# The sample's high and low parts side by side in one stationary operand

## The chip, the cores and the metric

The kernel runs on one core of a Trainium2 chip. The metric is the device time of one execution in microseconds (us). An execution is one inference step of one layer, for a prompt of 2048 frames and a sample of 64 frames that continues a running stream.

## The reference

A layer takes each frame of 1024 numbers, normalises it, and multiplies it with one wide input matrix. Its columns feed two branches and their gates. Branch A is a differential attention with four heads, branch B a retention with four heads. Both are gated, projected, merged and projected once more. Cut to what matters here:

```python
def layer_inputs(x, norm_g, w_in, b_gate, qn_g, kn_g):
    h = rmsnorm(x, norm_g) @ w_in              # (rows, 1024) @ (1024, W_IN)
    qa, ka, va, za, qb, kb, vb, zb, ga, gb = jnp.split(h, _split_points(), axis=-1)
    ...
def layer_output(x, oa, ob, za, zb, ga, gb, subln_g, lam_init, w_oa, w_ob, w_out):
    oa = (rmsnorm(oa, subln_g) * (1.0 - lam_init)).reshape(B, T, W_A) * jax.nn.silu(za)
    ob = rmsnorm(ob).reshape(B, T, W_B) * jax.nn.silu(zb)
    m = ga * (oa @ w_oa) + gb * (ob @ w_ob)
    return x + m @ w_out
def reference(...):
    # the same layer for the prompt (2048 rows) and for the sample (64 rows),
    # with the sample's attention over 4096 cached frames and its own 64
```

The outputs are y for prompt and sample, their attention keys and values, and the retention states.

## The kernel before, in words

Everything is float32. TensorE multiplies in a rounded form of it (F32R), so every operand is kept as a high part and a low part: the high part is the number rounded to that form, the low part is the rest. A product is three matmuls that add up in one accumulator: high times high, high times low and low times high. Low times low is left out.

A matmul has a stationary operand, which is loaded into the array (rows are the contraction, columns the rows of the output), and a moving operand, up to 512 columns wide. The accumulator is a bank of 128 partitions with 512 numbers each; its partitions are the stationary operand's columns.

The frames are taken in tiles of 128 rows. `x_tile` (L369) transposes a tile on TensorE and writes its high part `xh` (ScalarE) and its low part `xl` (VectorE), with eight contraction tiles of 128. The prompt's first half gives eight tiles; the sample is the ninth, with 64 rows. It stands in the columns 512 to 576 of the second segment.

There are two ways to project. In `natural` (L587) and `opening` (L510) the frames are stationary and the weights move, so the output has frames in its partitions. This is done for the values, keys and queries of the attention and for the values of the retention. In `transposed` (L749) the weights are stationary and the frames move. In both ways `mm_group` (L491) issues the three matmuls of each of the eight contraction tiles. For the attention's three projections in the first half of the frames the weights are 512 columns wide; for the retention's values there are two groups that are 256 wide. The sample is the last tile of each, with its 64 rows as 64 stationary columns: 24 matmuls in a group.

When a tile's matmuls are issued, an epilogue is started as a task of its own: `fin_qk` (L616), `fin_va` (L696) or `fin_vb` (L733). It reads the bank on ScalarE and VectorE, gives the bank (`mm`, two of them) back, and stores by DMA. The weights come by DMA in pieces of 256 KB (`ws`, three buffers); ScalarE makes the high part (L462) and GpSimd nearly all of the low parts (L472).

The last stage goes through eight groups of 256 prompt frames. `m_tile` (L1612) and `m_fin` (L1641) make the merged branches, as high and low part, for 256 columns of the prompt and eight of the sample; L1667 to L1670 collect the sample's eight in `self.ms`. `y_tile` (L1672) then multiplies a tile of 128 frames with the output matrix in two halves of 512 columns (two banks of `at`), three matmuls for each contraction tile (L1698 to L1700), and `y_fin` (L1707) adds the input and stores. After the eight groups one more `y_tile` does the sample, from `self.ms`.

The order of the work on TensorE, ScalarE and VectorE is set when the kernel is built: tasks run as coroutines under a clock that is estimated from each instruction's size, and the task of highest rank that is ready by that clock issues next. A buffer is taken with `take` and given back with `give` and an estimated time. Each engine carries out its instructions in the order in which they were issued. The order on GpSimd and on SyncE, which issues all the DMAs, is set by the framework's scheduler.

Of the kernel before, what the change touches and what calls it, by code (L numbers as in the profile page):

```python
# [60 lines left out]
class Hybrid:  # L61
# [307 lines left out]
    def x_tile(self, j, wait=True, mid=None):  # L369
        nc = self.nc  # L370
        yield lambda: len(self.xq) > j and self.xq[j] is not None
        xt, t, r, seg, col = self.xq[j]
        if wait:
            yield t
        self.until(t)
        for q in range(2):
            tag = "tp" if q == 0 else "pv"
            yield from self.take(tag)
            tp = self.psum(tag)
            for c in range(4):  # L380
                nc.tensor.transpose(tp[:, c * r:(c + 1) * r],
                                    xt[:, (4 * q + c) * 128:(4 * q + c + 1) * 128],
                                    self.ident[:r, :r])
# [4 lines left out]
            nc.scalar.copy(hi, pv)  # L388
            nc.vector.tensor_sub(lo, pv, hi.bitcast(F32))  # L389
# [101 lines left out]
    def mm_group(self, ps, n, us, wsl, x, wfirst, last, between=None):  # L491
        nc = self.nc
        seg, xsl = x
        for c in range(KC):
            a, b, _, tags, _ = yield from self.w_unit(us, c)
            a, b = a[:, wsl], b[:, wsl]
            xh, xl = self.xh[seg][:, c, xsl], self.xl[seg][:, c, xsl]
            ops = ((a, xh), (a, xl), (b, xh)) if wfirst else ((xh, a), (xh, b), (xl, a))
            for i, (p, q) in enumerate(ops):
                nc.tensor.matmul(ps, p, q, start=c == 0 and i == 0, stop=c == KC - 1 and i == 2)  # L500
                self.P(n)
            if last:
                for tag in tags:
                    self.give(tag, self.pe + LAT)
            if c % 2 and c < KC - 1:
                yield self.pe
                if between:
                    yield from between(c)

    def opening(self, fin):  # L510
# [4 lines left out]
        self.x_alloc(0)  # L515
        self.x_alloc(1)
        us, low = [], []
        yield lambda: len(self.xin) > 0
# [45 lines left out]
        for j in range(1, 9):  # L564
            def between(c):
# [4 lines left out]
                if c == 3 and j + 1 < 9:  # L570
# [4 lines left out]
                    if j + 2 < 9:  # L575
# [3 lines left out]
            yield from self.take("mm")  # L579
            ps = self.psum("mm")  # L580
            self.until(self.xt_ready[j])
            yield from self.mm_group(ps[:r], 512, us, slice(0, 512), (seg, slice(col, col + r)), False,
                                     j == 8, between)
            self.spawn(fin(ps[:r], r, 1, 128 * j if j < 8 else T, self.pe + LAT), 0, "w")
            yield self.pe

    def natural(self, half, fin, fresh=False, wide=False):  # L587
# [6 lines left out]
        for j0 in range(0, len(tiles), per):  # L594
# [3 lines left out]
            for u, (src, r, seg, col) in enumerate(group):  # L598
                if fresh:
                    yield lambda: len(self.xt_ready) > j0 + u  # L600
                    yield self.xt_ready[j0 + u]
                yield from self.mm_group(ps[:r, n * u:n * u + n], n, us, slice(0, n),
                                         (seg, slice(col, col + r)), False, j0 + u == len(tiles) - 1)
# [3 lines left out]
            self.spawn(fin(ps[:r, :n * len(group)], r, len(group), t0, self.pe + LAT), 0, "w")  # L607
            yield self.pe

    def rows_out(self, dst, src, nu, nbytes):  # L610
# [5 lines left out]
    def fin_qk(self, which, g, nh=2):  # L616
# [3 lines left out]

        def fin(ps, r, nu, t0, t):
            n, ng, rt = 128 * nh * nu, 2 * nh * nu, r * nu
# [11 lines left out]
            else:  # L634
                nc.vector.tensor_mul(raw3, ps.rearrange("p (g d) -> p g d", d=64),
                                     self.gk[:r].unsqueeze(1).to_broadcast([r, ng, 64]))
                t2 = self.V(n, t)
            self.give("mm", max(t1, t2))
            yield t1
# [56 lines left out]
    def fin_va(self, g, nh=2):  # L696
# [3 lines left out]

        def fin(ps, r, nu, t0, t):
            n, rt = 128 * nh * nu, r * nu
# [11 lines left out]
            t3 = self.V(n, t1)  # L714
            self.give("mm", max(t2, t3))
            if t0 < T:
# [16 lines left out]
    def fin_vb(self, g):  # L733
        nc = self.nc
        ep = self.ep

        def fin(ps, r, nu, t0, t):
            n, rt = 256 * nu, r * nu
# [3 lines left out]
            t = self.A(n, t)  # L742
            self.give("mm", t)
            yield t
# [896 lines left out]
    def m_fin(self, g, ct, pss):  # L1641
# [24 lines left out]
        yield t2 + 2000  # L1666
        for d, m in zip(self.ms, (h, l)):  # L1667
            nc.vector.tensor_copy(d[:, ct, 8 * g:8 * g + 8], m[:, 256:GW])
            t2 = self.V(8)
        self.msn.append(t2)  # L1670

    def y_tile(self, g, sel, r, x, y):  # L1672
# [3 lines left out]
        for nh in range(2):  # L1676
            nsl = slice(512 * nh, 512 * nh + 512)
            yield from self.take("xt")
            xt = self.sb(pb, [128, 512], "xt", "oxt")[:r]
            tx = self.ld(xt, x[:, nsl], 2048 * r)  # L1680
            yield from self.take("at")
            run.append((nsl, xt, tx, self.psum("at")[:r]))
        first = 8 if sel is None else 7
        order = [(c, k) for k in range(2) for c in range(first)] + [(c, k) for c in range(first, 8) for k in range(2)]
        for ct, nh in order:
            nsl, xt, tx, ps = run[nh]
            yield lambda: len(self.wout) > ct and nh in self.wout[ct][2] and len(self.mq[g]) > ct
            h, l, t = self.mq[g][ct]
            if sel is None:
                yield lambda: len(self.msn) == 64  # L1690
                t = max(t, self.msn[-1])
                h, l = self.ms[0][:, ct, :], self.ms[1][:, ct, :]
            else:
                h, l = sel(h), sel(l)
            wh, wl, tw = self.wout[ct]
            if max(t, tw[nh]) > self.pe:
                yield max(t, tw[nh])
            nc.tensor.matmul(ps, h, wh[:, nsl], start=ct == 0, stop=False)  # L1698
            nc.tensor.matmul(ps, h, wl[:, nsl], start=False, stop=False)  # L1699
            nc.tensor.matmul(ps, l, wh[:, nsl], start=False, stop=ct == 7)  # L1700
            for _ in range(3):
                t = self.P(512)
            yield self.pe
            if ct == 7:
                self.spawn(self.y_fin(ps, xt, y[:, nsl], r, max(t, tx)), 0)

# [12 lines left out]
    def out_stream(self):  # L1719
# [16 lines left out]
    def w_stream(self):  # L1736
# [53 lines left out]
        self.z4 = self.es.enter_context(self.tc.tile_pool(name="p3b", bufs=1))  # L1790
        self.ms = [self.z4.tile([128, 8, 64], F32R, tag=f"ms{j}", name=f"ms{j}") for j in range(2)]
        self.spawn(self.out_stream(), 8)
# [139 lines left out]
```

## Time and profile before

| | us |
|---|---|
| Median of 3 runs | 1988.08 |
| Lowest and highest | 1986.14, 1988.54 |
| The profiled execution | 1990.07 |
| Its span in the profile | 1988.3 |

The profile is of one execution. Its span runs from the first to the last instruction. A row of the timeline gives the start in the span, the duration, the engine, the line of the kernel, the operation, the tiles (output, then inputs), the shapes, a count, and in brackets how long the engine was idle before and for whom. Matmuls overlap, so a matmul's duration is longer than the distance to the next start; that distance, the step, is what counts for a busy TensorE. "128\*64" is the stationary operand: 128 contraction rows, 64 columns. A row of a group gives a count, then busy time in us and the mean of one in ns, then idle time before the group and who ended it. A row of DMA issues gives the count, the size of one and the median time from issue to landing. PE is TensorE, PEld its loads of stationary operands, DVE VectorE, ACT ScalarE, POOL GpSimd, SPq the queue of SyncE.

### The profile page before, as it was taken

The page shows a single profiled execution, that of the slowest core. Times are in us where ns is not written, and L with a number is a line of the kernel's source. Part 1 is how long each engine was busy: PE and PEld are TensorE (multiplying, and loading weights), DVE is VectorE, ACT ScalarE, POOL GpSimd, SP SyncE. Part 2 cuts the span into 40 slices and gives each one's busy share as a digit, 9 for nine tenths or more (in the row PEclk, how much of TensorE's full clock was granted, in tenths as well). Part 3 has the DMA queues.
Part 4 walks back from the last instruction along what each step waited for, and adds up shares of the span by engine and source line. Part 5 has one row for each costly group of instructions (what it writes and reads, how often), then busy time and mean ns, then how long its engine had stood idle before and what let it go on. Part 6 is the DMA issues. An engine that isn't in the chain of part 4 may idle for free.

```text
span 1988.3 us, 34106 instructions
## 1 busy us (share of the span) xinstructions
PE 1963.8 (99%) x12206; PEld 1754.7 (88%) x12206; DVE 1057.2 (53%) x2786; ACT 991.0 (50%) x2185; POOL 417.3 (21%) x383
## 2 busy tenths in 40 slices
PE   9999999999999999999999999999999999999999
PEld 7778989998998989999998888888888888889997
DVE  6453665446565326547756656525644356444432
ACT  6432666655454436436757656635744544333330
POOL 2310121212121221221111111211122434222210
PEclk9999999999999999999999999999999999999999
DMA  7646553335665756664352342652233666444431
GB/s 245 200 143 177 138 157 118 117 87 152 174 174 152 174 151 196 200 187 137 102 153 81 109 137 62 175 146 85 70 98 114 202 219 206 141 130 148 131 93 53
DMA packets 332508, 285.21 MB, mean 143 GB/s; under 512 B 65905, under 2 KB 297329, under 8 KB 332338
## 3 DMA queue, kind: packets, MB, share of 16 engines
q1 hardware_dynamic: 332338, 283.03, 48.5%
q8 instruction: 96, 1.57, 0.3%
q14 instruction: 74, 0.61, 0.1%
HBM read 187.19 MB, written 91.49 MB: 140 GB/s over the span
## 4 chain that ended last, share of the span: by engine, by line
PE 64%; DVE 2%; DMA 2%; ACT 1%; issue 0%; POOL 0%; SPq 0%; POOLq 0%; ACTq 0%; DVEq 0%
PE mm L500 31%; PE at L1698 3%; PE at L1699 3%; PE at L1700 3%; PE s L956 2%; PE s L957 2%; PE at L1063 2%; PE mm L1630 2%; PE s L1632 2%; PE mm L1631 2%; PE mm L1632 2%; PE s L1631 2%; PE s L1630 2%; PE pv L1043 1%; PE pv L1042 1%; PE pv L1041 1%
## 5 line engine op out<-in xcount | busy, mean ns | idle before, releaser
L500 PE MATMUL mm<-xh,wh 128*128 128x512 f32 (+2 forms) x1280 | 459.3, 359 | 2.8 <-ACT ev L770 2.8
L500 PE MATMUL mm<-xh,wl 128*128 128x512 f32 (+2 forms) x1280 | 452.4, 353 | 0.0
L500 PE MATMUL mm<-xl,wh 128*128 128x512 f32 (+2 forms) x1280 | 451.8, 353 | 0.0
L472 POOL TENSOR_TENSOR wl<-ws,wh 128x512 fp32r<-128x512 f32 x189 | 258.6, 1381 | 867.2 <-ACT wh L462 605.5
L500 PE MATMUL mm<-wh,xh 128*128 128x256 f32 (+3 forms) x864 | 273.5, 317 | 0.3 <-DVE tlo L713 0.3
L500 PEld LDWEIGHTS mm<-xh,wh 128*128 128x128 f32 x1280 | 241.4, 189 | 32.4 <-ACT ev L770 3.3
L500 PEld LDWEIGHTS mm<-xh,wl 128*128 128x128 f32 x1280 | 241.1, 188 | 31.9 <-POOL wl L472 0.4
L500 PE MATMUL mm<-wh,xl 128*128 128x256 f32 (+3 forms) x864 | 267.9, 310 | 0.1
L500 PE MATMUL mm<-wl,xh 128*128 128x256 f32 (+3 forms) x864 | 267.6, 310 | 0.0
L500 PEld LDWEIGHTS mm<-xl,wh 128*128 128x128 f32 x1280 | 241.6, 189 | 27.8
L1078 DVE TENSOR_TENSOR atl<-at,ath 128x512 fp32r<-128x512 f32 (+1 forms) x144 | 93.9, 660 | 159.2 <-ACT ath L1076 159.2
L500 PEld LDWEIGHTS mm<-wh,xh 128*128 128x128 f32 (+1 forms) x864 | 162.8, 188 | 11.8 <-PE s L957 0.4
L500 PEld LDWEIGHTS mm<-wl,xh 128*128 128x128 f32 (+1 forms) x864 | 162.9, 189 | 11.0
L500 PEld LDWEIGHTS mm<-wh,xl 128*128 128x128 f32 (+1 forms) x864 | 162.8, 188 | 10.9 <-DVE xl L389 0.6
L770 ACT COPY ev<-mm 128x512 f32<-128x512 f32 x140 | 71.3, 510 | 191.4 <-PE mm L500 166.4
L995 ACT ACTIVATE row<-row,a_mx 128x1024 f32<-128x1024 f32 (+7 forms) x160 | 153.3, 962 | 17.5 <-DVE a_mx L975 16.3
L965 DVE CUSTOM_DVE_ANT_0 row<-s,dfar 128x512 f32<-128x512 f32 (+2 forms) x192 | 118.2, 631 | 57.7 <-PE s L957 57.1
L462 ACT CAST wh<-ws 128x512 fp32r<-128x512 f32 x192 | 115.4, 618 | 33.2 <-PE mm L500 22.0
L1076 ACT CAST ath<-at 128x512 fp32r<-128x512 f32 (+1 forms) x144 | 78.6, 562 | 100.1 <-PE at L1063 95.2
L956 PE MATMUL s<-K,q 128*128 128x512 f32 (+3 forms) x320 | 118.3, 374 | 4.2 <-DVE a_acc L965 4.2
L957 PE MATMUL s<-K,q 128*128 128x512 f32 (+3 forms) x320 | 115.5, 362 | 0.0
L1016 DVE SCALAR_TENSOR_TENSOR row<-row,a_w 128x1024 f32<-128x1024 f32 (+4 forms) x96 | 102.6, 1074 | 21.5 <-ACT row L1013 21.4
(220 smaller groups left out, 3998.0 us busy)
## 6 DMA issues: line engine op xcount, KB each, us to landing
ws<-in_w_in_dram SPq DMA_DIRECT2D x192, 256.0 KB, 3.2
q<-qT SPq DMA_DIRECT2D x128, 128.0 KB, 3.0
V<-vN SPq DMA_DIRECT2D x24, 512.0 KB, 4.8
K<-kT SPq DMA_DIRECT2D x48, 256.0 KB, 4.1
gt<-gaT SPq DMA_DIRECT2D x64, 132.0 KB, 2.1
gt<-gbT SPq DMA_DIRECT2D x64, 132.0 KB, 2.1
xt<-in_x_prompt_dram SPq DMA_DIRECT2D x16, 512.0 KB, 5.9
kn<-in_cache_k_T_dram SPq DMA_DIRECT2D x32, 256.0 KB, 3.7
```

Source lines behind the costliest of these rows:

```text
L462: self.nc.scalar.copy(h, st)
L472: self.nc.gpsimd.tensor_sub(l, st, h.bitcast(F32))
L500: nc.tensor.matmul(ps, p, q, start=c == 0 and i == 0, stop=c == KC - 1 and i == 2)
L956: nc.tensor.matmul(ps, q1s, kk, start=True, stop=False)
L957: nc.tensor.matmul(ps, q2s, kk, start=False, stop=True)
L965: nc.vector.tensor_tensor_reduce(out=units[k0 // 1024][:, k0 % 1024:k0 % 1024 + n], in0=ps, in1=tab, scale=-SLOPES[h], scalar=3.0e38, op0= ...
L995: nc.scalar.activation(u, u, AF.Exp, bias=mx, scale=-1.0, accum_out=lp[:, k:k + 1])
L1016: nc.vector.scalar_tensor_tensor(out=u0, in0=u0, scalar=w[:, 0:1], in1=u1, op0=ALU.mult, op1=ALU.add)
L1078: nc.vector.tensor_sub(al[:, :w], at[:, :w], ah[:, :w].bitcast(F32))
L1630: nc.tensor.matmul(ps, wh[:, csl], oh, start=kt == 0, stop=False)
L1631: nc.tensor.matmul(ps, wh[:, csl], ol, start=False, stop=False)
L1632: nc.tensor.matmul(ps, wl[:, csl], oh, start=False, stop=kt == 3)
```

## The change

The sample's high and low part become the two halves of one stationary operand with 128 columns: `xs` for the projections, `ms` for the last output product. One matmul with the high part of the weights then gives high times high in the accumulator's partitions 0 to 63 and low times high in 64 to 127. A second matmul, with the sample's high part alone and the low part of the weights, adds to partitions 0 to 63. Three matmuls become two. The two halves of the accumulator have to be added afterwards: the lower half is brought to the partitions of the upper by a DMA within the on-chip memory, and added on VectorE.

In the projections `x_tile` fills `xs` with four copies on GpSimd. `mm_group` has a branch for 64 rows, in which the first contraction tile begins with the 128-column matmul and the others end with it. `halves` copies the bank with ScalarE, gives it back, moves the half, adds it, and then runs the old epilogue on the sum.

In the last product the sample's tile stands between the two last tiles of the prompt. Its input is loaded into buffers of another tag (`wst`), and `y_halves` takes the place of `y_fin`.

```diff
@@ x_tile
             self.give(tag, t2)
+            if r == 64:
+                for k, part in enumerate((hi, lo)):
+                    nc.gpsimd.tensor_copy(self.xs[:, 4 * q:4 * q + 4, 64 * k:64 * k + 64], part)
+                    t2 = self.G(256, t2)
@@ mm_group
+        if ps.shape[0] == 64:
+            both = self.both
         for c in range(KC):
...
             ops = ((a, xh), (a, xl), (b, xh)) if wfirst else ((xh, a), (xh, b), (xl, a))
+            if ps.shape[0] == 64:
+                pair = [(ps, xh, b), (both, self.xs[:, c, :], a)]
+                for i, (o, p, q) in enumerate(pair if c else pair[::-1]):
+                    nc.tensor.matmul(o, p, q, start=c == 0 and i == 0, stop=c == KC - 1 and i == 1)
+                    self.P(n)
+                ops = ()
@@ opening, natural
-            self.spawn(fin(ps[:r], r, 1, 128 * j if j < 8 else T, self.pe + LAT), 0, "w")
+            self.spawn_fin(fin, ps, r, 512, 1, 128 * j if j < 8 else T)
...
+    def spawn_fin(self, fin, ps, r, n, nu, t0):
+        t = self.pe + LAT
+        done = fin(ps[:r, :n], r, nu, t0, t) if r == 128 else self.halves(ps[:, :n], n, t, fin, t0)
+        self.spawn(done, 0, "w")
+
+    def halves(self, ps, n, t, fin, t0):
+        yield from self.take("ev")
+        up = self.sb(self.ep, [128, 512], "ev", "up")[:, :n]
+        self.nc.scalar.copy(up, ps)
+        t = self.A(n, t)
+        self.give("mm", t)
+        yield t
+        yield from self.take("tlo")
+        dn = self.sb(self.ep, [128, 512], "tlo", "dn")[0:64, :n]
+        t = self.ld(dn, up[64:128], 256 * n)
+        yield t
+        self.nc.vector.tensor_add(up[0:64], up[0:64], dn)
+        t = self.V(n, t)
+        self.give("tlo", t)
+        yield from fin(up[0:64], 64, 1, t0, t, "ev")
@@ y_tile
+            if sel is None:
+                pair = [(ps[:64], self.ms[:, ct, 0], wl[:, nsl]), (ps, self.ms[:, ct], wh[:, nsl])]
+                for i, (o, m, w) in enumerate(pair if ct else pair[::-1]):
+                    nc.tensor.matmul(o, m, w, start=ct == 0 and i == 0, stop=ct == 7 and i == 1)
+                    t = self.P(512)
...
+    def y_halves(self, ps, xt, y, r, t):
+        nc = self.nc
+        yield from self.take("wst")
+        yt = self.sb(self.z4, [128, 512], "wst", "oyt")
+        yield t
+        nc.vector.tensor_copy(yt[64:128], ps[64:128])
+        t2 = self.V(512, t)
+        nc.vector.tensor_add(xt, ps[0:64], xt)
+        t = self.V(512, t)
+        self.give("at", t)
+        yield t2
+        t2 = self.ld(yt[0:64], yt[64:128], 1 << 17)
+        yield t2
+        nc.vector.tensor_add(yt[0:64], yt[0:64], xt)
+        t = self.V(512, max(t, t2))
+        self.give("wst", t)
+        yield t
+        self.give("wst", self.st(y, yt[0:64], 2048 * r))
@@ out_stream
             for tt in range(2):
+                if g == 7 and tt:
+                    yield from self.y_tile(7, None, 64, self.i["x_sample"][0], self.o["y_sample"][0])
...
-        yield from self.y_tile(7, None, 64, self.i["x_sample"][0], self.o["y_sample"][0])
```

More of the change, by code (lines that the diff above doesn't have):

```diff
@@ L742, in fin @@
             t = self.A(n, t)
-            self.give("mm", t)
+            self.give(bank, t)
             yield t
@@ L1677, in y_tile @@
             nsl = slice(512 * nh, 512 * nh + 512)
-            yield from self.take("xt")
-            xt = self.sb(pb, [128, 512], "xt", "oxt")[:r]
+            tag = "xt" if sel else "wst"
+            yield from self.take(tag)
+            xt = self.sb(pb, [128, 512], tag, "oxt")[:r]
             tx = self.ld(xt, x[:, nsl], 2048 * r)
             yield from self.take("at")
-            run.append((nsl, xt, tx, self.psum("at")[:r]))
+            run.append((nsl, xt, tx, self.psum("at")))
         first = 8 if sel is None else 7
@@ L1790, in w_stream @@
         self.z4 = self.es.enter_context(self.tc.tile_pool(name="p3b", bufs=1))
-        self.ms = [self.z4.tile([128, 8, 64], F32R, tag=f"ms{j}", name=f"ms{j}") for j in range(2)]
+        self.ms = self.z4.tile([128, 8, 2, 64], F32R, tag="ms", name="ms")
         self.spawn(self.out_stream(), 8)
```

39 lines of the change are left out of this document (20 added, 19 removed).

## The prediction

> **What bounds the kernel now.** I read the head of the page first, then the busy time by stage, then what TensorE waited for.
>
> ```profile
> span 1988.3 us, 34106 instructions
> PE 1963.8 (99%) x12206; PEld 1754.7 (88%) x12206; DVE 1057.2 (53%) x2786; ACT 991.0 (50%) x2185; POOL 417.3 (21%) x383
> ```
>
> TensorE (PE) is busy in 1963.8 of 1988.3 us; VectorE (DVE) and ScalarE (ACT) in about half. A share of the whole hides stages, so here are those that hold the sample's matmuls (columns: stretch, its length, then busy time and count for each engine, the granted clock, DMA share, GB/s):
>
> ```profile
> 64.30:69.80 5.50, 5.50 (x25) 3.28 (x24) 0.69 (x1) 2.63 (x5) 1.82 (x2) 1.00 0.76 290
> 69.80:119.00 49.20, 48.27 (x225) 39.23 (x224) 25.60 (x67) 14.83 (x37) 8.45 (x7) 1.00 0.50 156
> 119.00:180.00 61.00, 60.86 (x289) 47.16 (x288) 31.80 (x74) 22.77 (x57) 7.61 (x6) 1.00 0.50 147
> 180.00:240.00 60.00, 60.00 (x483) 58.83 (x482) 27.78 (x104) 30.20 (x71) 5.82 (x5) 1.00 0.65 169
> 240.00:300.00 60.00, 58.50 (x385) 54.02 (x385) 41.18 (x129) 41.19 (x97) 13.40 (x11) 1.00 0.58 155
> 1961.60:1973.20 11.60, 11.43 (x50) 8.95 (x49) 1.48 (x4) 0.00 (x0) 0.00 (x0) 1.00 0.27 92
> 1973.20:1984.50 11.30, 11.24 (x48) 6.35 (x48) 1.33 (x3) 0.00 (x0) 0.00 (x0) 1.00 0.25 81
> 1984.50:1988.30 3.80, 0.00 (x0) 0.00 (x0) 0.66 (x1) 0.00 (x0) 0.00 (x0) 0.85 0.15 35
> ```
>
> In every one of them but the last 3.8 us TensorE is busy nearly all the time, at the full granted clock. From 240 to 300 us, where the other engines work hardest, DVE and ACT are busy 41 of 60 us. The sample's last product (1973.2 to 1984.5) is almost pure TensorE. What TensorE waited for in the whole span, longest first:
>
> ```profile
> PE tp L1452 <- DVE rru L1446: 4.4, 3, 1.6
> PE s L956 <- DVE a_acc L965: 4.2, 6, 1.5
> PE mm L500 <- ACT ev L770: 2.8, 2, 2.2
> ```
>
> No wait is over 4.4 us in total. So a matmul that is taken away should shorten the span by the distance from its start to the next start, as long as the new work round it stays beside TensorE.
>
> **The matmuls that go.** The sample has 64 rows, so its stationary operand has 64 columns, yet a pass takes as long as with 128. These are starts and durations of TensorE's matmuls at the edges of the sample's groups ("128*64" is rows and columns of the stationary operand):
>
> ```profile
> 64.08 0.39 PE L500 MATMUL mm<-wh,xl 128*128 128x512 f32 x1
> 64.31 0.40 PE L500 MATMUL mm<-wh,xh 128*64 128x512 f32 x1
> ...
> 69.82 0.40 PE L500 MATMUL mm<-wh,xh 128*128 128x512 f32 x1
> ...
> 202.26 0.28 PE L500 MATMUL mm<-wh,xh 128*64 128x256 f32 x1
> ...
> 204.99 0.28 PE L500 MATMUL mm<-wh,xh 128*128 128x256 f32 x1
> ...
> 206.31 0.28 PE L500 MATMUL mm<-wh,xl 128*128 128x256 f32 x1
> ```
>
> First wide group: 24 matmuls from 64.31 to 69.82, 5.51 / 24 = 0.230 us each. There are three wide groups (values, keys, queries of attention). Each goes from three passes per contraction tile to two, 8 passes fewer: 3 x 8 x 0.230 = 5.5 us. Two 256-wide groups (retention values): (204.99 - 202.26) / 24 = 0.114 us; with 128 columns (206.31 - 204.99) / 11 = 0.120. Eight go and eight become 128 wide: 8 x 0.114 - 8 x 0.006 = 0.86, twice 1.7 us.
>
> ```profile
> 1961.21 0.40 PE L1700 MATMUL at<-woh,ml 128*128 128x512 f32 x1
> ...
> 1961.69 0.50 PE L1698 MATMUL at<-woh,mh 128*128 128x512 f32 x1
> ...
> 1972.70 0.40 PE L1700 MATMUL at<-woh,ml 128*128 128x512 f32 x1
> 1973.19 0.45 PE L1698 MATMUL at<-woh,ms 128*64 128x512 f32 x1
> ...
> 1984.05 0.40 PE L1700 MATMUL at<-woh,ms 128*64 128x512 f32 x1
> ```
>
> Last output product: 47 steps from 1973.19 to 1984.05, 0.231 us each; 16 of 48 go, 3.7 us. **Together 10.9 us.**
>
> The tile before it runs from 1961.69 to 1972.70, 47 steps of 0.234. At both tile edges the step is 0.48 and 0.49 us, 0.25 more, since an accumulator bank has to be evicted first. With the sample's tile put between the last two prompt tiles, its first bank is done eight contraction tiles early, so the last prompt tile finds it free: one such edge goes, 0.25 us. The last prompt tile then covers the sample's own tail.
>
> **Switching between 64 and 128 columns.** The new order alternates: 128, 64, 64, 128, 64, 128 and so on, 14 changes in each of 7 groups (five projections, two banks of the output), 98, where before has about 13; 85 more. The fence above prices a change: 64.08 to 64.31 into 64 columns is 0.23, an ordinary step, and the way out to 128 columns at 69.82 is the last of the 24 steps that make 5.51, so it can hide no more than a few hundredths. I take nothing. A change in the number of rows is the nearest thing with a price:
>
> ```profile
> 60.44 0.40 PE L500 MATMUL mm<-wh,xl 128*128 128x512 f32 x1
> 60.77 0.46 PE L381 MATMUL tp<-ident,xt 64*128 64x64 f32 x4
> ```
>
> 0.33 us, 0.10 over a step. So 0 to 0.10 each, 0 to 8.5 us, and I take 0 because the rows with the very same counts of columns say so. [...]
>
> **The packed copies.** Four copies on GpSimd (POOL) fill the packed operand, behind the third of the weight splits below; the first matmul of the first group needs three of them (both high parts stand ahead of the low ones in POOL's order).
>
> ```profile
> 58.12 3.78 POOL L472 TENSOR_TENSOR wl<-ws,wh 128x512 fp32r<-128x512 f32 x3 [4.99 <-DMA vN<-tlo]
> ...
> 61.53 0.38 ACT L388 CAST xh<-pv 128x256 fp32r<-128x256 f32 x1
> ...
> 62.01 0.41 DVE L389 TENSOR_TENSOR xl<-pv,xh 128x256 fp32r<-128x256 f32 x1
> ...
> 67.98 3.79 POOL L472 TENSOR_TENSOR wl<-ws,wh 128x512 fp32r<-128x512 f32 x3 [6.08 <-ACT wh L462]
> ...
> L840 POOL TENSOR_TENSOR r_y<-r_y,r_sq 128x256 f32<-128x256 f32 x33 | 25.7, 777 | 275.4 <-DVE r_sq L837 207.7 <-PE mm L500 40.3 <-PE s L957 13.8
> L472 POOL TENSOR_TENSOR wl<-ws,wh 128x512 fp32r<-128x512 f32 x189 | 258.6, 1381 | 867.2 <-ACT wh L462 605.5 <-PE mm L500 129.5 <-PE s L957 48.9
> ```
>
> POOL is free at 61.90 and the high parts are there at 61.91. A copy has 128x256 elements, the size of the 777 ns row: three end at 61.91 + 2.33 = 64.24, just ahead of 64.31. No cost. If a copy took the 1381 ns of twice the size, three would end at 66.05 and TensorE would wait 1.7 us. So 0 to 1.7; I take 0, the row of the same size. POOL's next splits (67.98) wait for ACT anyway, so nothing is queued behind.
>
> **Bringing the halves together.** Rows 64 to 127 of the accumulator hold the low part's share. Per projection group there is now an ACT copy of the bank, a DMA of 64 rows within SBUF, a DVE add, and then the old epilogue on the sum.
>
> ```profile
> 66.79 0.59 ACT L711 COPY raw<-mm 128x512 f32<-128x512 f32 x1
> ...
> 69.31 2.81 SPq L136 DMA_DIRECT2D ws<-in_w_in_dram  x3
> ...
> 76.17 0.69 DVE L635 TENSOR_TENSOR raw<-mm,gk 128x512 f32<-128x512 f32 x1 [4.38 <-ACT sq L629]
> ...
> both<-row SPq DMA_DIRECT2D x16, 256.0 KB, 3.5
> vN<-thi SPq DMA_DIRECT2D x1, 128.0 KB, 3.3
> ```
>
> Copy 0.59, landing 3.3 to 3.5, add 0.69: about 5 us, five times. The sample's own bank comes free sooner, after one copy. What can hurt is the queue: ACT's next reading of the sum, and all behind it, stands until the add, and the transfer itself stands behind two weight loads on SP's queue. For the first group: the sample's matmuls now end at 64.31 + 16 x 0.230 = 67.99; two of the loads at 69.31 go first, so the transfer is issued near 71.0, lands near 74.3, is added by 75.0; ACT's two copies and a weight cast end by 76.7 (three times 0.59), and the next tile's bank is read by ACT and DVE by 78.0 (0.59 + 0.69). That bank is wanted again 48 steps after 67.99, at 79.0. One microsecond of slack, where before had 80.84 - 76.86 = 4.0 (48 steps after 69.82, against the end of the row at 76.17). So 0 to, say, 2 us in a group if a landing is slow; later groups have as much or more of TensorE's work beside them. I take 1.0 for all five. In the sample's last product the same round trip lies under the last prompt tile, 11 us long.
>
> **The order of the rest.** The shorter groups shift the planned order of attention and projection work as far as about 300 us; beyond that it is the same until the last tiles.
>
> ```profile
> 64.31:300.00 235.69, 233.11 (x1400) 202.52 (x1399) 127.05 (x373) 111.62 (x263) 37.10 (x30) 1.00 0.56 160
> ```
>
> TensorE idles 235.69 - 233.11 = 2.6 us there now. The new order can save these or double them: -2.6 to +2.6. I take 0.5, since one more chain hangs on each group.
>
> **The end.** Before ends with a 128 KB store of the sample, after with a 256 KB store of the prompt:
>
> ```profile
> out_y_prompt_dram<-oyt SPq DMA_DIRECT2D x32, 256.0 KB, 2.4
> out_y_sample_dram<-oyt SPq DMA_DIRECT2D x2, 128.0 KB, 2.3
> ```
>
> 0.1 us more.
>
> **Sum:** -10.9 - 0.25 + 0 + 1.0 + 0.5 + 0.1 = -9.5 us. The profiled execution took 1990.07 us (its span 1988.3 and 1.8 round it), so it would take 1980.5. The median of the runs is 1988.08, 2.0 below the profiled one; against it I forecast 1978.6 us, 0.48% faster. The gain is some four times the spread of the runs shown (2.4 us); 0.2% (4 us) is about what can be told from no change.
>
> **Rivals.**
> First, the column changes cost, and the kernel is slower. A matmul lasts 0.39 us against a step of 0.23, so an array that had to empty at each change would lose 0.16; 85 of them are 13.6 us, giving 1978.6 + 13.6 = 1992.2. It turns the sign from 9.5 / 85 = 0.11 us a change. Against it: the changes in the trace cost nothing; for it, only that none there come one right after another. Chance 0.08. At the 0.10 of the row change it would be 1987.1, no measurable change: 0.05.
>
> Second, the round trips are not covered: ACT and DVE stand behind them and TensorE waits for a bank. At 2 us in each of three wide groups (slack of 1 us exceeded by a landing of 6.3) it adds 5 over the 1.0 taken: 1983.6. Chance 0.10.
>
> Third, the change doesn't shorten the first 300 us, because chains of DVE, ACT and DMA set their length. Then only the end's 3.7 + 0.25 - 0.1 remain: 1984.2. Against it: TensorE idles 2.6 of 235.69 us. Chance 0.06.
>
> My own case has 0.71. Its range is 1975 (idle gone, no wait) to 1982. With the second and third rivals the range is 1975.0 to 1986.0, which leaves out the first. Faster 0.82 (the forecast less a little, with the second and third), same 0.09, slower 0.09.
>
> **What would show it.** In each wide group: 16 matmuls in about 3.7 us with steps of 0.23 through the changes of columns (0.33 or 0.39 would prove the first rival); the first of them at the same distance from its transposes (else the POOL copies are late); TensorE's idle time from 64 to 300 us near 3 us (over 8 would be the second rival); the sample's output in 7.4 us and no 0.48 step behind it; a last store that lands in 2 to 3 us. I am wrong if steps lengthen where columns alternate, or if a wait on the new add appears in the list of TensorE's waits with several microseconds.

## The result and the profile after

The changed kernel took 1982.71 us (median of 9 runs, 1981.03 to 1985.7), the kernel before 1988.11 us (9 runs, 1986.14 to 1991.79). The ratio is 0.997, with a 95% interval from 0.996 to 0.9981: 0.3% faster, 5.4 us. The forecast was 1978.6 us, 9.5 us faster. The sign held, and so did the range that takes in the rivals (1975.0 to 1986.0); the range of the case that was forecast (1975 to 1982) was left by 0.7 us. 4 us of the gain are missing. The profiled execution took 1983.19 us, its span 1981.4 us.

First the sample's first wide group, TensorE's timeline of the changed kernel (start, duration, engine, line, operation, tiles, shapes):

```profile
63.95 0.40 PE L512 MATMUL mm<-wh,xl 128*128 128x512 f32 x1
64.18 0.39 PE L508 MATMUL mm<-wh,xs 128*128 128x512 f32 x1
64.41 0.63 PE L508 MATMUL mm<-wl,xh 128*64 128x512 f32 x2
64.88 0.39 PE L508 MATMUL mm<-wh,xs 128*128 128x512 f32 x1
...
67.64 0.40 PE L508 MATMUL mm<-wh,xs 128*128 128x512 f32 x1
```

The 15 steps from 64.18 to 67.64 are 0.231 us each, through all changes between 128 and 64 columns. The group is 16 matmuls long instead of 24, and starts without a gap behind the tile before it. So the matmuls went as foreseen and the changes of columns cost nothing.

Now the stages of the changed kernel, as busy time by stretch (the columns are those of the prediction's second fence):

```profile
64.30:120.00 55.70, 51.61 (x230) 41.00 (x229) 28.28 (x68) 16.94 (x41) 10.13 (x8) 0.97 0.51 164
120.00:180.00 60.00, 59.27 (x284) 47.50 (x283) 30.36 (x72) 22.26 (x56) 8.52 (x6) 1.00 0.49 142
180.00:240.00 60.00, 60.00 (x482) 58.95 (x481) 29.14 (x105) 30.74 (x70) 5.83 (x5) 1.00 0.67 176
240.00:300.00 60.00, 60.00 (x388) 55.46 (x387) 39.44 (x133) 43.12 (x104) 14.11 (x11) 1.00 0.64 170
```

From 64 to 120 us TensorE now idles 55.70 - 51.61 = 4.1 us; before it was 0.9 from 64.3 to 119 (5.50 of 5.50 and 48.27 of 49.20 busy). The granted clock is 0.97, before 1.00. The stretch from 120 to 180 us idles 0.7, and the two behind it nothing, where before idled 1.5 from 240 to 300. The list of what TensorE waited for, over the whole span of the changed kernel, names the place (us in total, number of waits, the longest):

```profile
PE tp L703 <- DVE raw L688: 4.7, 3, 4.0
```

One wait of 4.0 us, on the transposes of a tile's keys. Its history, from the timeline of the changed kernel; first the transposes and the matmuls behind them on TensorE:

```profile
79.34 0.50 PE L512 MATMUL mm<-wh,xh 128*128 128x512 f32 x1
...
87.73 1.12 PE L703 MATMUL tp<-ident,raw 128*128 128x128 f32 x4 [4.04 <-DVE raw L688]
...
89.07 0.63 PE L512 MATMUL mm<-wl,xh 128*128 128x512 f32 x1
...
90.74 0.39 PE L512 MATMUL mm<-wh,xl 128*128 128x512 f32 x1
```

And what ScalarE, SyncE's queue and VectorE did before it:

```profile
70.88 0.50 SPq L136 DMA_DIRECT2D dn<-up  x1
...
75.69 0.68 DVE L641 TENSOR_TENSOR up<-up,dn 64x512 f32<-64x512 f32 x1 [7.70 <-DMA dn<-up]
76.41 0.62 ACT L745 CAST thi<-up 64x512 fp32r<-64x512 f32 x1 [3.95 <-DVE up L641]
...
78.60 0.69 DVE L671 TENSOR_TENSOR raw<-mm,gk 128x512 f32<-128x512 f32 x1 [0.85 <-ACT sq L665]
79.21 0.14 DVE L201 TENSOR_SCALAR gsub<-gsub 128x1 f32<-128x1 f32 x1
...
81.79 0.69 DVE L676 TENSOR_REDUCE ms<-sq 128x8 f32<-128x512 f32 x1
...
83.68 0.69 DVE L671 TENSOR_TENSOR raw<-mm,gk 128x512 f32<-128x512 f32 x1 [1.00 <-ACT sq L665]
...
84.29 1.23 DVE L233 SCALAR_TENSOR_TENSOR sm_t<-sm_y 128x8 f32<-128x8 f32 x1
85.56 1.19 DVE L234 TENSOR_TENSOR sm_t<-sm_t,ms 128x8 f32<-128x8 f32 x1
...
86.98 0.69 DVE L688 TENSOR_TENSOR raw<-raw,sm_y 128x512 f32<-128x512 f32 x1
```

The low half is issued at 70.88 and added at 75.69, 4.8 us later. VectorE stands for 7.70 us and ScalarE for 3.95, since the add and the two copies behind it are next in their queues, and the normalising of the next tile's keys is queued behind those. It ends at 87.67. The bank itself was nearly in time: the matmul that takes it begins at 79.34, 0.43 behind its neighbour instead of 0.23, so 0.2 us late. The transposes, which stand 18 matmuls later in TensorE's order, were 4.0 us late. In the kernel before the steps that answer to these were (timeline; the bank was read at 76.17):

```profile
76.78 0.68 DVE L640 TENSOR_REDUCE ms<-sq 128x8 f32<-128x512 f32 x1
...
77.96 0.14 DVE L201 TENSOR_SCALAR gsub<-gsub 128x1 f32<-128x1 f32 x1
...
81.08 0.69 DVE L652 TENSOR_TENSOR raw<-raw,sm_y 128x512 f32<-128x512 f32 x1
...
81.92 0.63 PE L667 MATMUL tp<-ident,raw 128*128 128x128 f32 x4 [0.93 <-DVE raw L652]
```

There TensorE waited 0.93 us. Now the keys are ready 5.9 us later (87.67 against 81.77), and TensorE, with the transposes planned further back, comes only 2.7 us later (idle from 83.69 against 80.99): 0.93 + 5.9 - 2.7 = 4.1, about the 4.04 seen.

Of the 5.9 us, 2.4 come from the later reading of the bank (78.60 against 76.17). The other 3.5 arise behind it in VectorE's queue. A set of small constants (L201 to L217, 79.21 to 81.78) now stands ahead of the reduction L676; before, it stood behind the reduction, and two steps of ScalarE that the keys need ran beside it. The reading of the second tile of keys (83.68) now stands ahead of L233. And L205 (79.57, 1.21 us) and L234 took 1.2 us each, where before they took 0.2.

The wait has a second price. The same kernel, busy time by stretch:

```profile
87.70:89.06 1.36, 1.33 (x5) 1.25 (x6) 0.74 (x2) 0.18 (x1) 0.00 (x0) 0.50 0.62 180
89.06:90.80 1.74, 1.74 (x6) 1.38 (x5) 0.69 (x1) 0.72 (x3) 0.00 (x0) 0.53 0.66 234
90.80:94.00 3.20, 3.20 (x16) 2.39 (x15) 2.10 (x6) 0.60 (x1) 0.00 (x0) 1.00 0.43 129
```

Behind the wait the granted clock is 0.50 for some 3 us. From 89.07 to 90.74 four steps take 1.67 us, 0.42 each instead of 0.23. The whole piece from the transposes (87.73) to 90.74 takes 3.01 us; the kernel before has the same piece in about 1.6 us (transposes at 81.92, the next matmuls at 82.31, 82.62 and 82.85, and three more steps of 0.23). So about 1.4 us more: the wait cost 5.4 us in all, 4.5 more than the 0.93 of the kernel before. The clock fell to 0.50 at 87.27 us, 3.6 us into the idle time, and was back at 1.00 at 90.68; in the kernel before, with 0.93 us of idle time, it was 1.00 throughout (82 to 86 us). The price isn't the same in every execution. In a second profile of the changed kernel (`after_again`, below) the same wait, of 3.99 us, is followed by a slow stretch about twice as long (the mean clock from 64.3 to 130 us is 0.95 there, 0.97 in the first profile):

```profile
86.90:92.10 5.20, 5.17 (x14) 4.22 (x15) 2.23 (x6) 1.50 (x4) 0.00 (x0) 0.50 0.65 204
```

The eleven steps from its transposes (86.93) on take 5.18 us there, before 2.78 (81.92 to 84.70), 2.4 more: 6.4 us in all.

At the end the output part did what it should. TensorE's timeline of the changed kernel:

```profile
1958.93 0.50 PE L1735 MATMUL at<-woh,ms 128*128 128x512 f32 x1
...
1966.41 0.39 PE L1739 MATMUL at<-woh,mh 128*128 128x512 f32 x1
...
1977.32 0.40 PE L1741 MATMUL at<-woh,ml 128*128 128x512 f32 x1
```

The sample takes 1966.41 - 1958.93 = 7.5 us, and the last prompt tile begins one ordinary step (0.23) behind it.

### The profile page after: what moved, and what is told of

It reads as the page before. It is cut to its first block, busy times and chain, and to the rows that moved or that the text cites. A ratio compares the mean times of both kernels' runs of the same rounds, so it can differ in the third digit from the quotient of the medians.

```text
span 1981.4 us, 34021 instructions
## 1 busy us (share of the span) xinstructions
PE 1955.7 (99%) x12150; PEld 1752.6 (88%) x12150; DVE 1056.9 (53%) x2795; ACT 994.1 (50%) x2190; POOL 420.6 (21%) x387
## 4 chain that ended last, share of the span: by engine, by line
PE 65%; DVE 2%; issue 1%; ACT 1%; DMA 1%; POOL 0%; SPq 0%; POOLq 0%; ACTq 0%
PE mm L512 32%; PE at L1739 3%; PE at L1740 3%; PE at L1741 3%; PE s L992 2%; PE s L993 2%; PE at L1099 2%; PE mm L1666 1%; PE mm L1667 1%; PE s L1668 1%; PE mm L1668 1%; PE s L1667 1%; PE s L1666 1%; PE pv L1079 1%; PE pv L1078 1%; PE pv L1077 1%
## 5 line engine op out<-in xcount | busy, mean ns | idle before, releaser
L512 PE MATMUL mm<-wh,xh 128*128 128x256 f32 (+1 forms) x824 | 259.4, 315 | 0.8 <-ACT raw L668 0.5
L512 PE MATMUL mm<-wl,xh 128*128 128x256 f32 (+1 forms) x824 | 253.5, 308 | 0.5 <-POOL wl L476 0.5
L512 PE MATMUL mm<-wh,xl 128*128 128x256 f32 (+1 forms) x824 | 253.5, 308 | 0.0
L512 PEld LDWEIGHTS mm<-wh,xh 128*128 128x128 f32 x824 | 157.0, 191 | 10.6 <-ACT raw L668 0.7
L512 PEld LDWEIGHTS mm<-wl,xh 128*128 128x128 f32 x824 | 157.1, 191 | 9.4 <-POOL wl L476 0.7
L512 PEld LDWEIGHTS mm<-wh,xl 128*128 128x128 f32 x824 | 156.9, 190 | 8.2 <-DVE xl L389 0.2
```

## The experiments

Each kernel below ran beside the kernel before on the same chip, which took 1988.34, 1987.88 and 1987.74 us in the three sets. Two theories stood at the start. **A**: the missing gain is lost in the first hand-over (the values), where the add holds the queues of ScalarE and VectorE; the rest of the projections gained what it should. **B**: the loss is spread over the later stages, and the first hand-over has no special part in it.

**The output part alone.** The projections are as before; only the sample's last product is changed. (The diffs from here on are against the changed kernel; "..." stands for lines left out.)

```diff
@@ mm_group, x_tile, opening, natural: as in the kernel before
-            if ps.shape[0] == 64:
-                pair = [(ps, xh, b), (both, self.xs[:, c, :], a)]
...
-            self.spawn_fin(fin, ps, r, n * len(group), len(group), t0)
+            self.spawn(fin(ps[:r, :n * len(group)], r, len(group), t0, self.pe + LAT), 0, "w")
```

> Only the last output product is changed, with its place before the last prompt tile; the projections are those of before. Theory A (the loss is a stall behind the first hand-over of halves in the projections, near 88 us): nothing of that is here, so the whole gain of this part shows, 16 steps of 0.231 us and one edge of 0.25 less 0.1, about -3.9 us against the kernel before (1984.2), and TensorE waits 0.9 us before L667 at 82 us as in before. Theory B (the loss is spread over the later stages, where the trace after has lost 1.5 us between 344 and 1958 us): this part also gives less than -3.9, some -2.5 us.

It took 1983.51 us, ratio 0.9977 (0.9969 to 0.9986): 4.8 us gained, of 3.85 foreseen. B expected less than 3.9, so this speaks against it. The total is only 0.8 us above that of the changed kernel, but that doesn't mean that the projections bring so little. All three profiles have one and the same wait of 2.2 us, on `ev`; the matmul that ends it starts at 490.10 us in the kernel before, at 490.64 here and at 485.93 in the changed kernel. By then the projections have brought over 4 us. This kernel then gains elsewhere: a wait of 1.6 us that the kernel before has at 806 us doesn't come up in it. The next run separates the theories better.

**The first group as before.** The sample's values in the opening group use the old three passes and the old epilogue. The other four groups and the output stay changed.

```diff
@@ opening
-            ps = self.both = self.psum("mm")
+            ps, self.both = self.psum("mm"), None
...
-            self.spawn_fin(fin, ps, r, 512, 1, 128 * j if j < 8 else T)
+            self.spawn(fin(ps[:r], r, 1, 128 * j if j < 8 else T, self.pe + LAT), 0, "w")
```

> The whole change, except that the sample in the first wide group (attention values) goes by the old three passes and the old epilogue (the four packed copies remain for the other groups). Theory A: the 4 us wait of the transposes near 88 us and the halved clock behind it (together about 5.5 us) are gone, and 8 steps of 0.23 come back: 5.5 - 1.8, so 3.7 us faster than the change, about 1979.0 us. Theory B: only the 8 steps come back, 1.8 us slower than the change, about 1984.5.

It took 1977.45 us, ratio 0.9946 (0.9932 to 0.9959), though eight matmuls (1.8 us) are back. Its busy time by stretch:

```profile
64.30:120.00 55.70, 55.70 (x259) 44.18 (x258) 27.60 (x70) 19.31 (x45) 11.83 (x10) 1.00 0.52 168
```

TensorE is never idle there. B, which expected 1984.5, falls; A, which expected 1979.0, is borne out: the changed first group costs about 1982.7 - 1977.5 + 1.8 = 7 us more than its matmuls alone would. The wait and the slow clock behind it are 5.4 to 6.4 us of this by the two profiles; the rest is less than the measurements can resolve.

**A later place in the plan.** The hand-over's task gets an estimated landing 8 us later, so that the planner puts the add, and all that depends on it, behind the next tile's epilogue. The transfer itself isn't touched; only the place in the queues changes.

```diff
@@ halves
-        t = self.ld(dn, up[64:128], 256 * n)
+        t = self.ld(dn, up[64:128], 256 * n) + 8000.0
```

> The whole change; only the planner's estimate of when the moved half lands is 8 us later, so that ACT and DVE do the next tile's epilogue ahead of the sample's add. Theory A: the wait before the first key transposes falls from 4.0 us to 1 us or less and the clock stays whole, so 4 to 5.5 us faster than the change, 1977 to 1978.7 us. Theory B: within 1 us of the change.

A miss: 1982.25 us, ratio 0.9971 (0.996 to 0.9981), no better than the changed kernel. TensorE's waits in this kernel:

```profile
PE s L992 <- DVE a_acc L1001: 4.5, 6, 1.9
PE tp L703 <- DVE raw L688: 3.9, 3, 2.2
```

The wait of 4.0 us is gone, and two of about 2 us stand elsewhere: 2.2 us near 132 us and 1.9 near 252, where the changed kernel idles 0.7 us from 120 to 180 us and not at all from 240 to 300.

**The constants later as well.** In the changed kernel a set of small VectorE operations, the constants of the differential attention (L201 to L217, 79.2 to 81.8 us), stands between the add and the keys. Here they move away too.

```diff
@@ consts
-        yield t + 12000
+        yield t + 40000
@@ halves
-        t = self.ld(dn, up[64:128], 256 * n)
+        t = self.ld(dn, up[64:128], 256 * n) + 8000.0
```

> As late8, and the small lambda constants on DVE (2.6 us of DVE's queue between the first key tile's reading and its reduction) are planned 28 us later as well. Theory A: no wait at the first key transposes; as late8 or up to 1 us faster, 1977 us. If the constants and not the moved half were what counts, this is faster than late8 by 2 us or more.

A miss again: 1982.39 us, ratio 0.9972 (0.9961 to 0.9983). With the add already out of the way, the constants make no difference to the sum; moving them alone in the changed kernel was not tried. Where the loss went is seen in the timeline of this kernel, at the second hand-over (the keys):

```profile
130.24 0.60 ACT L665 ACTIVATE sq<-mm 128x512 f32<-128x512 f32 x1 [4.21 <-DMA ws<-in_w_in_dram]
...
133.71 0.63 PE L703 MATMUL tp<-ident,raw 128*128 128x128 f32 x4 [2.86 <-DVE raw L688]
...
135.77 0.67 DVE L641 TENSOR_TENSOR up<-up,dn 64x512 f32<-64x512 f32 x1
```

The low half of the keys was issued at 120.49 us and landed at 124.8. Its buffer is one of only two called `tlo`, which the prompt's tiles need for their squares and for the low parts of their own keys and queries. With the add delayed to 135.77 it is held for 15 us, and the epilogues of the prompt's tiles share the one that is left; I read ScalarE's pause of 4.21 us before 130.24 as theirs, though the profile puts it down to a weight load: the square at 130.24 goes into a `tlo`, and the other one held the low part of a tile's keys, whose store was issued at 125.28 and landed 4.8 us later, at 130.1. Hence **theory A2**: two things cost, the place of the first add in the queues, and the `tlo` buffer held during a hand-over that lasts long.

**Later in the first hand-over only.** The values' epilogue, the first, gets the 8 us; keys, queries and the retention's values don't.

```diff
@@ spawn_fin
-        done = fin(ps[:r, :n], r, nu, t0, t) if r == 128 else self.halves(ps[:, :n], n, t, fin, t0)
+        done = fin(ps[:r, :n], r, nu, t0, t) if r == 128 else self.halves(ps[:, :n], n, t, fin, t0, 8000.0 * (self.both is ps))
@@ halves
-        t = self.ld(dn, up[64:128], 256 * n)
+        t = self.ld(dn, up[64:128], 256 * n) + late
```

> The whole change; the moved half is planned 8 us later in the first hand-over alone (attention values), in the other four as in the change. Theory A2 (there is a cost at every hand-over: the add and what follows it stand in the queues of ACT and DVE, and the moved half holds one of two tlo buffers until the add; planned late, the first is cured and the second gets worse, as in late8): here the wait near 88 us goes and the one near 134 us does not come, so TensorE idles about 5 us less between 64 and 130 us than in the change, 1977.5 us. Rival C (the order in which the planner puts the transposes is what counts, and any shift of it makes a new wait somewhere): 1981 to 1983 us as late8.

1975.72 us, ratio 0.9938 (0.9925 to 0.995): 7.0 us faster than the changed kernel, where A2 said 5, and the same 7 us that the old first group gave. The rows that answer to those of the changed kernel, from this kernel's timeline:

```profile
79.66 0.66 PE L703 MATMUL tp<-ident,raw 128*128 128x128 f32 x4 [0.99 <-DVE raw L688]
80.07 0.47 PE L512 MATMUL mm<-wh,xh 128*128 128x512 f32 x1
```

The transposes wait 0.99 us, about as in the kernel before (0.93), and the piece behind them starts as quickly as there (0.41 to the next matmul, before 0.39): no slow clock (1.00 from 64.3 to 130 us). The same add stands later (at 81.58), and TensorE doesn't wait for it. That the gain comes from here, and not from a better order of the later work, is seen at the wait of 2.2 us named above. The matmul that ends it, in the changed kernel:

```profile
485.93 0.50 PE L512 MATMUL mm<-xh,wh 128*128 128x512 f32 x1 [2.25 <-ACT ev L806]
```

and in this one:

```profile
479.54 0.51 PE L512 MATMUL mm<-xh,wh 128*128 128x512 f32 x1 [2.24 <-ACT ev L806]
```

6.4 us earlier, of which 0.4 stood at the start of the first group already (63.81 against 64.18). From 348 to 1100 us TensorE idles 8.9 us here, about as in the changed kernel (9.5).

**Another buffer.** The low half goes into a buffer of another tag, `row`, so that no `tlo` is held.

```diff
@@ halves
-        yield from self.take("tlo")
-        dn = self.sb(self.ep, [128, 512], "tlo", "dn")[0:64, :n]
+        yield from self.take("row")
+        dn = self.row("dn")[0:64, :n]
...
-        self.give("tlo", t)
+        self.give("row", t)
```

> The whole change; the moved half goes into a row buffer of the attention (ten of them) instead of one of the two tlo buffers, planned as in the change. Theory A2: the first hand-over's wait near 88 us comes from the queues and stays (3 to 5 us), the second is no worse: 1981 to 1983 us. Rival D (the tlo buffer alone is the cause): the wait goes, 1977.5 us.

The wait stayed, as A2 said (3.45 us at 84.18), but the time did not: 1976.63 us, ratio 0.994 (0.9927 to 0.9952), 6 us better than the changed kernel. **Both edits**, the other buffer and the 8 us in all hand-overs:

> The moved half in a row buffer and planned 8 us later in all five hand-overs. Theory A2: neither the wait near 88 us nor the one near 134 us, about 5 us faster than the change: 1977.5 us. Rival C: a wait of 2 us or more turns up elsewhere before 300 us, 1981 us or more.

1973.02 us, ratio 0.9925 (0.9913 to 0.9937). The buffer takes away what the delay had brought in `late8`: its longest wait on a tile's keys is 1.4 us. A2 was right about the waits, but said 1977.5: the time is 4.5 us better. **The old first group and the other buffer** (the edits of the second and the sixth experiment):

> The first wide group by three passes, the other four in two with the moved half in a row buffer. Theory A2: the four hand-overs that are left have no wait that a buffer would cure, so as first_old within 1 us: 1976.5 to 1978.5 us.

1977.01 us, ratio 0.9947 (0.9935 to 0.9958): the buffer adds nothing here.

So one surprise was left: what the buffer brings while the wait stays. A last set has the four cells of the two edits side by side on one chip, the changed kernel itself among them.

> The changed kernel itself, unedited, so that it stands on the same chip as the next three, which together are the four cells of two edits: the low half in the row buffer (yes or no) and the estimated landing 8 us later (yes or no). If what is measured of each edit is the edit's own, this one gives 1982 to 1983.5 us, 0.9970 of the kernel before.

> Row buffer alone. Theory A2 (only the wait near 85 us and the one behind the tlo buffer cost anything) had 1981 to 1983 and the first measurement was 1976.6. If the first measurement was the chip and not the edit, this is within 2 us of the unedited kernel beside it. If the buffer itself is worth something without the later landing, it is 4 to 7 us faster than the unedited kernel, though its wait near 85 us is still 3 to 5 us long.

> Later landing alone. First measured at 1982.25. By A2 it has exchanged the wait near 88 us for one at the second hand-over, so it is within 1.5 us of the unedited kernel beside it.

> Both edits. First measured at 1973.0. If the two edits act on different places, its distance to the unedited kernel is at least the sum of the two single distances: 8 to 10 us faster. If the first measurement was the chip, 4 to 6 us.

| | low half in `tlo` | low half in `row` |
|---|---|---|
| planned as written | 1982.55 (0.9972, 0.9963 to 0.9982) | 1975.36 (0.9939, 0.9925 to 0.9953) |
| 8 us later | 1981.88 (0.9974, 0.9965 to 0.9983) | 1971.70 (0.9921, 0.9907 to 0.9934) |

All four repeat within 1.4 us. The buffer alone is worth 7.2 us, the delay alone 0.7, both 10.9: so the buffer's gain is the edit's own, and not the chip's. Where it lies is seen far from the hand-overs. Busy time from 348 to 1100 us in the changed kernel:

```profile
348.00:700.00 352.00, 349.17 (x2178) 318.26 (x2178) 178.09 (x439) 180.05 (x414) 73.29 (x56) 1.00 0.53 145
700.00:1100.00 400.00, 393.37 (x2966) 374.70 (x2965) 240.88 (x640) 223.74 (x482) 77.03 (x59) 1.00 0.51 151
```

and with the other buffer:

```profile
348.00:700.00 352.00, 350.70 (x2195) 318.38 (x2194) 173.45 (x424) 174.26 (x400) 73.28 (x54) 1.00 0.53 147
700.00:1100.00 400.00, 396.54 (x2977) 379.49 (x2976) 242.66 (x644) 228.47 (x491) 78.24 (x60) 1.00 0.50 150
```

TensorE idles 9.46 us there in the changed kernel and 4.76 with the other buffer, 4.7 us less; in the profiles of the last set it is 9.1 and 4.7. TensorE's waits from 300 to 1100 us show which ones went. The changed kernel:

```profile
PE mm L512 <- ACT ev L806: 2.8, 2, 2.2
...
PE tp L1488 <- DVE rru L1482: 1.3, 1, 1.3
PE pv L381 <- DVE xl L389: 0.9, 1, 0.9
```

With the other buffer:

```profile
PE mm L512 <- ACT ev L806: 1.2, 2, 0.7
PE s L992 <- DVE a_acc L1001: 0.8, 3, 0.3
```

The planner took another order on TensorE, ScalarE and VectorE from about 80 us on, and in that order the wait of 2.2 us near 486 us and those of 1.3 and 0.9 between 740 and 790 us don't come up. That is 4.4 to 4.7 of the buffer's 7.2 us. The 2.2 us wait is followed by a slow clock in some executions (below), worth another 1.6 us where it was measured; the rest is within what the measurements can resolve. The first measurement and its repeat show the same short list. The kernel before has the wait of 2.2 us as well (in the prediction's list of waits), so this is no loss of the change undone: it is a better order of work that the change doesn't touch. `first_old_row`, which gained nothing from the buffer, has the 2.2, 1.3 and 0.9 us waits still. That the waits went with the new order is shown; why the planner came upon that order from a buffer's availability was not traced.

The version with both edits, at 1973.0 and 1971.7 us, is faster than either kernel: by 0.75 and 0.79% than the kernel before.

## Why the prediction was right in sign and too good by 4 us

- **The matmuls that go** (10.9 us): right. The first group's steps are 0.231, and the output took 7.5 us. With the first add out of the way the kernel gains 12.2 us (`va_late`, 1987.88 - 1975.72), of which 1.5 is a wait near 251 us that only the kernel before has. One small cost was not foreseen: the step out of the first group, 67.64 to 68.05, is 0.41, since the shorter group ends as the bank of the tile ahead of it is still being read (L749, to 68.00).
- **The edge** (0.25): right, an ordinary step at 1966.41.
- **Switching between 64 and 128 columns** (0, up to 8.5): 0 was right, 0.231 us a step through all changes. The first rival falls.
- **The packed copies** (0, up to 1.7): 0 was right, and the estimate was on the dear side. POOL's rows of the changed kernel:

```profile
62.00 0.74 POOL L394 CAST xs<-xh 128x256 fp32r<-128x256 f32 x2
```

Two copies take 0.74 us, 0.37 each against the 0.78 taken, and the other two, as long, are done at 63.44, before the 64.18 at which they are wanted.
- **Bringing the halves together** (1.0 in all, 0 to 2 in a group): this step failed. "One microsecond of slack" was worked out for one resource, the bank, and for a landing at 74.3. The landing took longer, as the view of that one transfer in the changed kernel shows:

```profile
DMA to landing us min/median/max: 4.7/4.7/4.7
```

The next tile's bank was read by 79.29 instead of 78.0, and that alone cost the 0.2 us seen. What was not looked at is that the same queues also carry the next tile's normalising, whose result TensorE takes at a fixed place. The kernel before had no slack there: its transposes already waited 0.93 us. The later reading of the bank, the landing's 1.4 us (4.7 instead of 3.3) included, brings 2.4 of the keys' 5.9 us. L205 and L234, stretched from 0.2 to 1.2 us each, bring 2.0, and the changed order of VectorE's queue the rest. These parts are read from the trace; they were not tried apart. In place of the 1.0 us taken, the hand-overs cost 4.5 us more than before at this wait, slow clock included (5.5 in the second profile); two experiments give about 7 for the whole. The other four hand-overs, which the term also covered, show at most the 0.7 us of idle time from 120 to 180 us. The right rule was there in the prediction ("what can hurt is the queue"), but it was applied to the first taker of the queue alone.
- **The second rival** (round trips not covered, 1983.6, chance 0.10) came nearest. Its mechanism, ScalarE and VectorE standing behind the hand-over, is what happened; its place was another, one group instead of three and the transposes instead of a bank. The prediction's own sign of being wrong, a wait on the new add of several microseconds, came in substance: the list shows 4.7 us for L688, which stands behind the add in VectorE's queue. The test set for it, TensorE's idle time from 64 to 300 us over 8 us, didn't fire: it was about 4.8 us (4.09 and 0.73 in the first two stretches), since the slow clock counts as busy (1.33 of 1.36 us from 87.70 on, at 0.50). **The third rival** gave nearly the same time (1984.2) for a wrong reason; the old first group at 1977.45 us refutes it, and so do the 4 us that the changed kernel is ahead at 486 us.
- **The order of the rest** (0.5, -2.6 to 2.6): inside its range, but of the other sign up to 348 us, where TensorE idles 0.7 us from 120 us on against 1.9 before. This was luck, and it hides about 1 us of what the first hand-over cost. From 348 to 1100 us the two are alike (9.5 against 9.3), but the premise that the order stays the same beyond 300 us holds only for that one plan. With one buffer renamed it moved by 4.7 us between 348 and 1100 us.
- **The end** (0.1): the span ends 4.1 us behind the start of the last matmul (1977.32 to 1981.4), before 4.25 (1984.05 to 1988.3). Right within 0.3.

## What to carry to other kernels

When a change puts a round trip in an engine's queue, go down that queue to every later result that TensorE takes at a fixed place, and give each its own slack; the first resource that comes free is not always the first that is late. Where before already waits a little at such a place, whatever delay the plan doesn't move back is paid in full (here 5.9 - 2.7 us), and a wait that the clock drops behind is paid with a surcharge (here 1.4 us in one profile and 2.4 in the other). And in a kernel whose order is planned from estimates, try the edit under two or three plans (another buffer, another estimated time): here two edits that change no arithmetic were worth 10.9 us, on top of the 5.4 of the change as written.

## What the runs showed of the hardware

- The granted clock was halved behind some waits of about 2 us, and not behind others. In the changed kernel, near 486 us, busy time by stretch:

```profile
483.60:485.93 2.33, 0.08 (x1) 0.00 (x1) 1.43 (x5) 2.27 (x8) 0.00 (x0) 1.00 0.52 102
487.00:490.00 3.00, 3.00 (x9) 2.32 (x8) 2.94 (x4) 0.76 (x2) 3.00 (x3) 0.50 0.77 190
```

and in the second profile of the same kernel (`after_again`), behind the same wait:

```profile
483.60:486.05 2.45, 0.21 (x2) 0.00 (x0) 1.43 (x5) 2.39 (x8) 0.00 (x0) 1.00 0.54 107
486.05:490.00 3.95, 3.95 (x17) 3.30 (x18) 3.81 (x7) 1.84 (x4) 3.40 (x3) 1.00 0.77 180
```

In the first, the slow stretch begins 0.7 us after TensorE has resumed and lasts 3.4 us (0.50 from 486.63 to 490.04). The twelfth matmul behind the wait starts 4.22 us after the first (490.15 against 485.93), in the kernel before 2.65 (492.75 against 490.10): 1.6 us more. In the second profile there is no slow stretch, and none behind this wait in the kernel before either (1.00 from 490.10 to 494.00). In the profile of the kernel before and the first of the changed kernel TensorE waits five times for over 1.6 us, behind the first 64 us. Half clock, for 3.4 us each time, came with three of these waits: 4.04 us (changed kernel, to 87.73; from 87.27 on), 2.25 (changed kernel, to 485.93; from 486.63 on) and 1.88 (before, to 982.70; from 983.64 on). It didn't come with 2.24 (before, to 490.10) and 1.88 (changed kernel, to 979.48), nor with the six waits of 1.28 to 1.58 us. In `both_later` it followed the wait of 2.86 us (0.50 from 134.95 to 138.00). Whether it follows a wait of about 2 us differed from execution to execution of the same kernel.
- VectorE's operations on 128x8 elements took 1.23 and 1.19 us (L233 and L234 above) while GpSimd ran two weight splits (from 84.23, 2.49 us for both), and the next one, L235 at 86.78, took 0.17 us. So each small operation lasted about as long as one split (2.49 / 2 = 1.25 us). What made them long was not shown by a run.
- In the changed kernel a transfer of 128 KB within SBUF (the low half of the values, a wide group) took 4.7 us from issue to landing, with weight loads on both sides of it in the same queue (69.19 and 71.70); the two of 64 KB (the 256-wide groups, issued at 211.9 and 245.6) took 2.1 and 3.6. In `first_old`, which has no such transfer for the values, those of the other groups took from 2.1 to 3.8 us.
